# Turning B, K and V to token rows in one RWKV-7 / Conformer / MLP layer: the transposing mode of the tensor engine replaced by ordinary products with the identity

## The chip, the cores and the metric

One core of one Trainium2 chip runs the whole layer in one launch. The metric is the device time of an execution in microseconds; lower is better. The kernel before was timed three times.

## The reference, cut to what matters

640 tokens (512 latent, 128 context) of width 1024 pass through one layer:

```python
xn = _rmsnorm(x, norm1_g) * (1 + sc1) + sh1
proj = xn @ w_in                                    # r k v | conv inputs | gates
y_r = _rwkv_branch(...)                             # 8 heads of 64, two directions
y_c = _conv_branch(...)                             # GLU, depthwise conv of 31, LayerNorm, swish
x = x + g1 * ((sigmoid(gate_r) * y_r + sigmoid(gate_c) * y_c) @ w_o)
x = x + g2 * (square(relu(xn2 @ mlp_w1)) @ mlp_w2)

def step(S, inp):                                   # the scan inside the RWKV branch
    rt, wt, kt, vt, at, bt = inp
    sa = einsum('bhvk,bhk->bhv', S, at)
    S = S * wt[:, :, None, :] + sa[..., None] * bt[:, :, None, :] + vt[..., None] * kt[:, :, None, :]
    return S, einsum('bhvk,bhk->bhv', S, rt)
```

Everything is float32. Large products are done as three passes over operands split into two parts (`hi` and `lo`, type float32r); small ones are plain float32 products.

## The kernel before, in words

Channels lie on the 128 partitions, tokens along the free axis, in two halves of 320. The program has three stretches. First the statistics, the modulation and the low-rank projections. Then "phase 1": all projections of the modulated input (dense products, 128x128 weights times 128x320 inputs, tiles `ps_mm<-xh_t,wh_t` and the like), with the RWKV branch and the conv branch running between them. Last the output projection and the MLP, dense products alone.

The scan doesn't run token by token. For each pair of heads (four pairs, `p`) the tokens of each direction are cut into 20 chunks of 32. The jobs of a pair are:

- `operands` writes the decayed operands, B and K as tile `BK`, with channels on partitions.
- `gram` (L769) makes inner products of every chunk: for each chunk two products of 64x64, one per head, `ps_a<-ARGH_t,BK_w` or `ps_b<-ARGH_t,BK_w`. Head 0 lies on partitions 0 to 63 and writes partitions 64 to 127 of the PSUM bank; head 1 the other way.
- `inverse` solves a triangular system per chunk.
- `turn` (L892) makes copies of B and K with the tokens on the partitions (tile `BKt`): a product of each chunk's `BK` block as the weights with the identity as the moving operand, `ps_a<-cst_t,BK_w` or `ps_b<-cst_t,BK_w`. It has the same two heads on the same corners of the array as `gram`. Four chunks times two heads are issued together; ScalarE then copies the bank to `BKt`.
- `fold` (L924) multiplies with the inverse.
- `chain` (L1020) is the scan itself, 20 steps. At each step `values` (L990) turns the V of one chunk of each direction and head: four products with the identity, `ps_a<-cst_t,vS_w` and `ps_a<-cst_t,vr_w`.

Both kinds of product with the identity ask `turned_to` (L209) whether they may use the tensor engine's transposing mode. It answers yes where the output starts at partition 0: in `turn` that is head 1 of the pair, in `values` one of the four products (head 1, direction 1).

What sets the order: phase 1 is written out by a planner that runs when the program is built. Every job is a generator (a "lane") with an urgency; the loop at the end of phase 1 asks for the first lane that can go on, and puts dense products in wherever none can. It keeps its own clock of each engine (`now`, `free`). The method `mm` (L192) moves that clock for each product and counts columns for the array's clock; a product in the transposing mode counts as 2 cycles a column, any other float32 product as 4:

```python
cyc = math.prod(rhs.shape[1:]) * (1 if rhs.dtype == F32R else 2 if "is_transpose" in kw else 4)
```

The order that results is fixed for TensorE, VectorE and ScalarE; DMAs are queued on SyncE.

Of the kernel before, what the change touches and what calls it, by code (L numbers as in the profile page):

```python
# [17 lines left out]
P = 128  # L18
# [17 lines left out]
TTILES = (0, 128, 192)  # first of the 128 tokens of each tile of a half  # L36

# [20 lines left out]
NWR, NWH = 2, 3  # halves of weights on the way, and split ones  # L58
# model of the engines' times (us) that sets the order of issue in phase 1
YG, YT, YF = 4, 4, 4  # L60
LEAD, SEM, LOAD = 0.40, 0.2, 4.0
BURST, REFRESH = 0, 15.0  # products without others between, now and then (us), that bring it back to full rate
# urgency of the lanes (the lowest first)
URGENT = dict(scan=0, split=0.3, shift=1.45, post=1, side=0.9, solve=1, prep=1.5, lora=2, ada=4, out=4.5, branch=0.5, conv=1.6)
# least times (us) between products of a lane whose results leave by a DMA, or whose weights come by one
GAP_LORA, GAP_ADA = 1.5, 3.5
V_STEP = 20  # of the scan after which the projection of V that takes its place may be planned
GLU_AT = 12  # their place among the projections
TICK, ENTRY, QUOTA, CREDIT, DEBT = 3.413, 3060, 1.55, 200, 6000  # clock gate of the tensor engine: columns in a tick that keep it at full rate
CST_ID, CST_MASK, CST_SEL, CST_HSEL, CST_LATE = 0, 128, 256, 258, 260  # L70
NCST = 261
# blocks of K = 1024 weights, in the order of the packed array
# [4 lines left out]
def hybrid_step(ctx: ExitStack, tc: tile.TileContext, I, O):  # L77
# [8 lines left out]
    # Estimates of the engines' times, in us. Instructions of the tensor engine are issued at now[0].  # L86
# [3 lines left out]
    class Timed:  # L90
        """an engine that counts the time of its instructions"""
# [67 lines left out]
    late = cst[:, CST_LATE:CST_LATE + 1]  # 1 on the second half of each 32 partitions  # L159
# [9 lines left out]
    # products of nothing in particular bring the tensor engine's clock to its full rate  # L169
# [6 lines left out]
    hw0 = st([P, 16], "hw0")  # halves of decay_w0 and iclr_a0  # L176
    ka2 = st([P, 8], "ka2")   # k_a / 2 and 1 - k_a / 2
# [3 lines left out]
    def derive():  # L181
        """derived parameters"""
# [9 lines left out]
    def mm(out, lhsT, rhs, start=True, stop=True, **kw):  # L192
# [3 lines left out]
        overlap = 128 // m if m < 128 else 128 // rhs.shape[0]  # products in different rows or columns of the array  # L196
# [12 lines left out]
    def turned_to(q):  # L209
        """for a product with the identity: the transposing mode writes from partition 0 only"""  # L210
        return {} if q else dict(is_transpose=True)

    def split(hi, lo, src):
        """src = hi + lo, each with the mantissa of one float32r pass."""
        A.activation(hi, src, AF.Copy)
        V.tensor_tensor(out=lo, in0=src, in1=hi.bitcast(F32), op=ALU.subtract)

    # halves of weights: planned, on the way, split; tags of free places for raw and split ones, and of those in use
# [4 lines left out]
    def place(free_, b):  # L223
        """whether there is a free place for a half of block b; those of phase 1 are not for the blocks after it"""
        while free_ and free_[0] not in ("wr", "wh") and b >= B_WO:
            free_.popleft()
        return len(free_) > 0

    def prefetch():
        """load the next halves of weights"""  # L230
# [14 lines left out]
    def take():  # L245
        """split the next half of a weight"""
# [40 lines left out]
    def mm3(ps, w, xh, xl, n0, n1, ks, first=True, last_=True):  # L287
        """ps += W^T X over the k tiles ks of a half w of W (k0 ... of X): hi hi + hi lo + lo hi; yields after each k tile."""
# [21 lines left out]
    def dense(xh, xl, evac, k0=0, k1=KD, pre=None):  # L310
        """the next block of weights (k tiles k0 ... k1) times X; evac(h, a, b, psum) takes each token half.
        Yields whether the tensor engine has got something."""
# [26 lines left out]
    def root(r, ps, scale, op, c):  # L339
        """r = op(scale * ps, c) ** -0.5"""  # L340
        if op == "max":
            V.tensor_scalar(out=r, in0=ps, scalar1=c, scalar2=None, op0=ALU.max)
        else:
            V.tensor_scalar(out=r, in0=ps, scalar1=scale, scalar2=c, op0=ALU.mult, op1=ALU.add)
        G.tensor_tensor(out=r, in0=r, in1=mhalf[0:r.shape[0], 0:r.shape[1]], op=ALU.pow)

    def inv_rms(srcs, h, scale, c, tg, bc):
        """(scale * sum over channels of srcs + c) ** -0.5 for token half h, spread over the channels; bc(psum) takes it."""
# [13 lines left out]
    def inv_norm(src, scale, op, c, tg, bc):  # L362
        """op(scale * sum of src over the channels of each head, c) ** -0.5, spread over the head's channels;
        bc(a, b, psum) takes it."""
# [15 lines left out]
    csb = st([P, 2 * KD + 30], "csb")  # 32 columns from 2 k on: c and c_ctx first, the rest is not used  # L380
# [6 lines left out]
    def ada(cols, tag, raws):  # L387
        """columns of mod: silu(c) @ ada_w + ada_b, transposed; raws: (k0, k1, tile) of the weights"""
# [21 lines left out]
    amod = st([P, 16, 2], "amod")  # norm_g * (1 + scale)  # L410

    def modulate(xt, k, rs, norm, segs, xh, xl, r0=0):
        """tile k of segments of the modulated input, split; rs: from token r0 on"""
# [82 lines left out]
    halves.extend((B_RKV + 4, j) for j in range(2))  # of the first product of phase 1  # L496
# [11 lines left out]
    # low-rank inner activations  # L508
# [13 lines left out]
    def lora2(p):  # L522
        """outer products of the low-rank pairs: tanh halves of decay and rate, and the gate; to DRAM"""
        def product(which, a, b, outs):
            """rows, function and place of the result of each product"""
# [13 lines left out]
        for which in range(2):  # L539
            for a, b in HALVES:  # L540
                outs = []
                for d in range(2):
                    back = which == 0 and d == 1  # direction 1 of the decay runs backwards through the tokens
# [17 lines left out]
    def proj_shift(kind, p):  # L561
        """r, k or v of head pair p with the token shift."""
# [74 lines left out]
    def bsum(src, tags, out_f):  # L637
        """sums over the 64 channels of each head, spread over them."""
# [10 lines left out]
    def hold():  # L649
        """one lane at a time has the two banks"""  # L650
        while held[0]:
            yield 0.2
        held[0] = True
# [10 lines left out]
    def operands(p):  # L664
        """decayed, normalised operands of the chunks: A | R into ARGH, B and K into BK"""
# [19 lines left out]
        for d in range(2):  # L685
# [5 lines left out]
            # decay and in-context rate; direction 1 runs backwards through the tokens  # L691
# [51 lines left out]
    BKt = wt([P, 2, NY, 64], "BKt")  # B and K with the tokens on the partitions, over and under an identity  # L743
# [12 lines left out]
    # Units of a pair: head parity s and direction d. Channel rows of a unit: 64 s ... The other half holds  # L756
    # its U and V (B and K) rows, U in quadrant 2 (1 - s) + d and V in the other quadrant of that half.
# [11 lines left out]
    def gram(p):  # L769
        """masked inner products of every chunk into ARGH; raw ones of B and A into Gf; then the decay of a chunk onto BK"""  # L770
# [33 lines left out]
    def inverse(p):  # L804
        """N[t, chunk, s] = ((I - G)^-1)[t, s], by blocked forward substitution, one chunk per lane; to Gf
        (the lanes without a chunk keep a zero strict triangle)"""
# [7 lines left out]
        def mulred(jobs):  # L814
            """out[a, b] = sum_s g[a, b, s] n[a, b, s] of each job (out, g, n, dims)"""
# [23 lines left out]
        T21 = G2[:, 16:24, 0:16].rearrange("p s (i j) -> p i s j", i=2)  # (the part of G that is not used here)  # L839

        def merge(blocks, n, jb):
            """N21 = N22 G21 N11 for the blocks of size n at blocks"""
# [21 lines left out]
        # the blocks of 16 on the tensor engine: rows t of every unit in its quadrant  # L864
# [24 lines left out]
    # chunks of direction 0 and 1 from which groups of scan steps start, and their numbers of steps  # L889
    GROUPS = (((16, 0), 4), ((0, 4), 8), ((8, 12), 8))  # L890

    def turn(p):  # L892
        """B and K with the tokens on the partitions: rows of a head in the other half; and V backwards.
        A group of steps takes the place of the one of the last pair."""
        BK = grp[p]["BK"]
        for g, (c0, n) in enumerate(GROUPS):
# [4 lines left out]
            for i, ds in enumerate([(0, 1)] if n == 4 else [(0,), (1,)]):  # L901
                yield max(0.0, ends[-2] - now[0])
                ps = bank(BANKS[i]).rearrange("p (y c) -> p y c", c=64)
                for y in range(8):
                    at = 20 * ds[y // n] + c0[ds[y // n]] + y % n
                    for s in range(2):
                        lo, o = 64 * s, 64 - 64 * s
                        mm(ps[o:o + 64, y, :], BK[lo:lo + 64, at, :], ident[lo:lo + 64, lo:lo + 64], **turned_to(o))
# [15 lines left out]
    def fold(p):  # L924
        """N^T into the B rows of the state update and of the output"""
# [37 lines left out]
    def solve(p):  # L963
# [10 lines left out]
        if p == 3:  # the places of the inverse can have weights  # L974
# [3 lines left out]
    # rings of the scan: state, U and V rows  # L978
# [5 lines left out]
    def cidx(c, i):  # L984
        """chunk of each direction at step i of the latent ('l') or context ('c') scan"""
# [4 lines left out]
    def values(p, n):  # L990
        """the V rows of a step"""
        S, ps = SVU[p % 2][n % 2], grp[p]["ps"]
        for s, d in UNITS:
            lo, q, t = 64 * s, vq(s, d), 32 * cidx(*STEPS[n])[d]
            mm(ps[q:q + 32, d, :], (vr if d else rk[2, p])[lo:lo + 64, t:t + 32], ident[lo:lo + 64, lo:lo + 64],
               tile_position=(lo, q), **turned_to(q))
# [4 lines left out]
    def output(p, n):  # L1001
        """the outputs of a step"""
# [17 lines left out]
    def chain(p):  # L1020
# [14 lines left out]
        for n in range(20):  # L1035
# [14 lines left out]
            if n == 3:  # the latents start from the given states  # L1050
# [12 lines left out]
            end = S if n == 3 else Sn  # of the context: a result  # L1063
# [13 lines left out]
    def post(p):  # L1077
        """group norm of each head, bonus and gate; to DRAM"""
        y0, y = grp[p]["Y"], rk[2, p]  # V is not needed any more
# [572 lines left out]
```

## Time and profile before

| | |
|---|---|
| three timed runs | 1401.06, 1413.18, 1482.34 us |
| median | 1413.18 us |
| span of the profiled execution, first to last instruction | 1416.9 us |
| mean granted TensorE clock in it | 0.901 |
| TensorE products (PE), weight loads (PEld) | 1370.3 us (97%), 1165.0 us (82%) |
| VectorE (DVE), ScalarE (ACT), GpSimd (POOL) | 740.5 us (52%), 551.8 us (39%), 28.9 us (2%) |

The profile gives the span of its execution, not a time with what lies around it. Columns of a group's row: line, engine, operation, output and inputs, shapes, count of records, then busy us and mean ns of one, then the engine's idle time before them. In a timeline row the first number is the start in us from the span's start and the second the duration of the merged piece. In a row of stretches each engine has its busy us with the number of its records behind it, then come the granted clock (1.00 is full), the DMA share and GB/s. Line 193 is the matmul call in `mm` and line 106 the call through which VectorE, ScalarE and GpSimd instructions are recorded, so the tiles tell which instruction is meant.

### The profile page before, as it was taken

To read this page: it belongs to the slowest core of one execution; us is meant where nothing else is said; L and a number is where in the kernel's file an instruction comes from. 1 tells how busy PE (TensorE), PEld (TensorE's weight loads), DVE (VectorE), ACT (ScalarE), POOL (GpSimd) and SP (SyncE) were. 2 spreads that over 40 slices of the span, in tenths; PEclk is the share of its full clock that TensorE was granted. 3 is DMA by queue.
4 is the path that set the end of the run, shared out by engine and by line. 5 is a ranking of instruction groups with operands and counts; after the bars stand their busy time and mean duration, and the time that the engine had idled before them with its cause. 6 is when DMAs were issued, how large, how long until landed. Compare 5 with 4: busy or idle time off the path is not lost.

```text
span 1416.9 us, 31247 instructions
## 1 busy us (share of the span) xinstructions
PE 1370.3 (97%) x13122; PEld 1165.0 (82%) x13122; DVE 740.5 (52%) x1606; ACT 551.8 (39%) x1390; POOL 28.9 (2%) x21
## 2 busy tenths in 40 slices
PE   8999999999999999999999979999999999999997
PEld 5776677677777677776777879999999999999997
DVE  5445557663856557543574356565443343344344
ACT  4555336542644226422265522334442242242130
POOL 0100000000000000000000000000000000000000
PEclk9999869996988679655799999999999999999998
DMA  9455223120421134121322167321222222222222
GB/s 373 142 173 185 82 65 119 60 76 34 132 84 56 42 123 141 48 67 40 104 85 67 43 206 267 119 75 46 75 75 75 75 75 75 75 75 75 75 82 75
DMA packets 82572, 140.38 MB, mean 99 GB/s; under 512 B 17024, under 2 KB 31616, under 8 KB 82432
## 3 DMA queue, kind: packets, MB, share of 16 engines
q1 hardware_dynamic: 82432, 138.39, 29.4%
q8 instruction: 103, 1.69, 0.5%
q14 instruction: 37, 0.30, 0.1%
HBM read 113.52 MB, written 22.22 MB: 96 GB/s over the span
## 4 chain that ended last, share of the span: by engine, by line
PE 91%; DMA 4%; DVE 2%; issue 2%; ACT 1%; SPq 0%; POOL 0%; POOLq 0%; DVEq 0%; ACTq 0%
PE ps_mm L193 47%; PE ps_b L193 25%; PE ps_a L193 10%; PE ps_t L193 7%; PE ps_ad L193 3%; DMA adl_w<-in_adal 2%; DMA adar_s<-in_adaw 1%; DMA z<-tmp 1%; ACT tmp L106 0%; DVE kk_t L106 0%; DVE ARGH_t L106 0%; DVE vS_w L106 0%; DMA pg_t<-g 0%; DVE wl_t L106 0%; DVE rS_w L106 0%
## 5 line engine op out<-in xcount | busy, mean ns | idle before, releaser
L193 PE MATMUL ps_mm<-xh_t,wh_t 128*128 128x320 f32 x656 | 235.5, 359 | 2.0 <-ACT tmp L106 1.7
L193 PE MATMUL ps_mm<-xh_t,wl_t 128*128 128x320 f32 x656 | 232.2, 354 | 0.0
L193 PE MATMUL ps_mm<-xl_t,wh_t 128*128 128x320 f32 x656 | 230.9, 352 | 0.0
L106 ACT ACTIVATE svu_w<-ps_a 64x128 f32<-64x128 f32 x320 | 87.1, 272 | 171.5 <-PE ps_a L193 166.0
L193 PEld LDWEIGHTS ps_mm<-xh_t,wh_t 128*128 128x128 f32 x656 | 136.1, 208 | 21.1 <-issue 11.5
L193 PEld LDWEIGHTS ps_mm<-xl_t,wh_t 128*128 128x128 f32 x656 | 136.8, 209 | 15.2 <-issue 10.2
L193 PEld LDWEIGHTS ps_mm<-xh_t,wl_t 128*128 128x128 f32 x656 | 136.5, 208 | 13.6 <-issue 7.4
L106 ACT ACTIVATE wh_t<-wr_t 128x512 fp32r<-128x512 f32 x147 | 92.4, 629 | 138.7 <-PE ps_b L193 107.1
L106 DVE TENSOR_TENSOR wl_t<-wr_t,wh_t 128x512 fp32r<-128x512 f32 x147 | 100.9, 688 | 82.2 <-ACT wh_t L106 76.8
L106 DVE TENSOR_TENSOR svu_w<-ps_b,Dc_w 64x128 f32<-64x128 f32 x152 | 43.7, 288 | 80.8 <-PE ps_b L193 78.0
L106 DVE SCALAR_TENSOR_TENSOR cacc_w<-upad_w,par_t,cacc_w 128x640 f32<-128x640 f32 x90 | 79.2, 880 | 2.0 <-ACT cacc_w L106 0.2
L193 PE MATMUL ps_mm<-ARGH_t,wh_t 128*128 128x320 f32 x252 | 71.0, 321 | 2.7 <-ACT wh_t L106 1.7
L106 ACT ACTIVATE tmp<-ps_mm 128x320 f32<-128x320 f32 x80 | 34.8, 436 | 88.7 <-PE ps_mm L193 88.5
L193 PE MATMUL ps_mm<-ARGH_t,wl_t 128*128 128x320 f32 x196 | 63.1, 322 | 5.0 <-DVE wl_t L106 5.0
L106 ACT ACTIVATE BKt_w<-ps_a 32x512 f32<-32x512 f32 (+3 forms) x80 | 40.0, 503 | 55.8 <-PE ps_a L193 54.8
L106 ACT ACTIVATE mwh<-wr_t 128x512 fp32r<-128x512 f32 x49 | 30.9, 632 | 73.3 <-PE ps_b L193 69.9
L106 DVE TENSOR_TENSOR tmp<-tmp 128x320 f32<-128x320 f32 x64 | 31.2, 489 | 43.6 <-ACT tmp L106 43.5
L106 DVE TENSOR_TENSOR mwl<-wr_t,mwh 128x512 fp32r<-128x512 f32 x49 | 33.7, 690 | 37.9 <-ACT mwh L106 37.9
L106 DVE SCALAR_TENSOR_TENSOR ARGH_t<-ps_mm,mod_t,ARGH_t 128x320 f32<-128x320 f32 (+2 forms) x45 | 22.6, 511 | 57.9 <-PE ps_mm L193 57.9
L193 PE MATMUL ps_a<-cst_t,BK_w 64*64 64x64 f32 x288 | 52.2, 282 | 0.0
L193 PEld LDWEIGHTS ps_mm<-ARGH_t,wh_t 128*128 128x128 f32 x252 | 47.5, 199 | 3.8 <-ACT wh_t L106 1.9
L193 PEld LDWEIGHTS ps_a<-cst_t,BK_w 64*64 64x64 f32 x288 | 33.1, 146 | 20.5 <-issue 3.9
(374 smaller groups left out, 3156.7 us busy)
## 6 DMA issues: line engine op xcount, KB each, us to landing
wr_t<-in_w SPq DMA_DIRECT2D x222, 256.0 KB, 2.8
adl_w<-in_adal SPq DMA_DIRECT2D x64, 256.0 KB, 2.8
adar_s<-in_adaw SPq DMA_DIRECT2D x16, 512.0 KB, 8.4
ARGH_t<-in_x SPq DMA_DIRECT2D x8, 640.0 KB, 6.3
z<-tmp SPq DMA_DIRECT2D x32, 160.0 KB, 2.8
gate<-tmp SPq DMA_DIRECT2D x32, 160.0 KB, 2.1
tA_t<-z SPq DMA_DIRECT2D x8, 320.0 KB, 3.1
ath_t<-z SPq DMA_DIRECT2D x8, 320.0 KB, 4.8
```

Source lines behind the costliest of these rows:

```text
L106: return f(*args, **kw)
L193: PE.matmul(out=out, lhsT=lhsT, rhs=rhs, start=start, stop=stop, **kw)
```

## The change

`turned_to` is gone, and the two calls that used it pass nothing. All products with the identity in `turn` and `values` are ordinary float32 products, for both heads. Everything else in the diff is removed comments, which are left out here.

```diff
-    def turned_to(q):
-        """for a product with the identity: the transposing mode writes from partition 0 only"""
-        return {} if q else dict(is_transpose=True)
-
...
-                        mm(ps[o:o + 64, y, :], BK[lo:lo + 64, at, :], ident[lo:lo + 64, lo:lo + 64], **turned_to(o))
+                        mm(ps[o:o + 64, y, :], BK[lo:lo + 64, at, :], ident[lo:lo + 64, lo:lo + 64])
...
             mm(ps[q:q + 32, d, :], (vr if d else rk[2, p])[lo:lo + 64, t:t + 32], ident[lo:lo + 64, lo:lo + 64],
-               tile_position=(lo, q), **turned_to(q))
+               tile_position=(lo, q))
```

Because the planner counts the two modes differently, the written order changes too. TensorE in the first `turn` of the first pair (`BK_w` are B and K, `cst_t` the identity, `ps_a` the bank, `x8` four chunks of two heads), before:

```order
L193 MATMUL ps_mm<-xl_t,wh_t 128x320
L193 MATMUL ps_mm<-xh_t,wl_t 128x320
L193 MATMUL ps_a_1767<-cst_t,BK_w 64x64 x8
L193 MATMUL ps_mm<-xh_t,wh_t 128x320
L193 MATMUL ps_mm<-xl_t,wh_t 128x320
L193 MATMUL ps_a_1767<-cst_t,BK_w 64x64 x8
L193 MATMUL ps_mm<-xh_t,wl_t 128x320
```

These seven rows read the same in the changed program: here nothing moved, and a `turn` batch is eight products in both.

A little later on TensorE the orders part. Around a weight load for the modulation (`ps_ad<-adl_w,csb_t`, four products) stands, before:

```order
L193 MATMUL ps_mm<-xh_t,wh_t 128x320
L193 MATMUL ps_mm<-xl_t,wh_t 128x320
L193 MATMUL ps_mm<-xh_t,wl_t 128x320
L193 MATMUL ps_ad<-adl_w,csb_t 32x128 x4
L193 MATMUL ps_mm<-xh_t,wh_t 128x320
```

and in the changed program:

```order
L193 MATMUL ps_mm<-xh_t,wh_t 128x320
L193 MATMUL ps_mm<-xl_t,wh_t 128x320
L193 MATMUL ps_ad<-adl_w,csb_t 32x128 x4
L193 MATMUL ps_mm<-xh_t,wl_t 128x320
L193 MATMUL ps_mm<-xh_t,wh_t 128x320
```

The small products moved ahead of one dense product.

On ScalarE, where the first pair's scan begins (`ARGH_t` and `BKt_w` are written by `fold`, `svu_w` by the scan, `wh_t` is a split weight, `u_t` and `rS_w` are the evacuated projection of r), before:

```order
L106 ACTIVATE BKt_w<-ps_a_2366 32x512
L106 ACTIVATE mod_t<-ps_ad,par_t 128x2
L106 ACTIVATE BKt_w<-ps_a_2366 32x512
L106 ACTIVATE svu_w<-ps_a_2390 64x2x64 x2
L106 ACTIVATE BKt_w<-ps_a_2366 32x512 x2
L106 ACTIVATE svu_w<-ps_a_2390 64x2x64 x4
L106 ACTIVATE tmp<-ps_mm 128x320
```

and in the changed program:

```order
L106 ACTIVATE BKt_w<-ps_a_2363 32x512
L106 ACTIVATE ade_t<-ps_ad 128x128
L106 ACTIVATE wh_t<-wr_t 128x512
L106 ACTIVATE BKt_w<-ps_a_2363 32x512 x3
L106 ACTIVATE svu_w<-ps_a_2358 64x2x64 x8
L106 ACTIVATE Y_w<-ps_t 128x32 x2
```

The scan's first copies (`svu_w`) moved behind the last of `fold`'s copies of that group, and one more split of a weight stands ahead of them. From there on, pieces of a few instructions differ all through phase 1; the counts of batches (40 of eight in `turn`, 80 of four in `values`) don't.

## The prediction

> **What bounds the kernel now.** I read the page's busy table first, then its slices, then its chain.
>
> ```profile
> span 1416.9 us, 31247 instructions
> PE 1370.3 (97%) x13122; PEld 1165.0 (82%) x13122; DVE 740.5 (52%) x1606; ACT 551.8 (39%) x1390; POOL 28.9 (2%) x21
> ...
> PEclk9999869996988679655799999999999999999998
> ...
> PE 91%; DMA 4%; DVE 2%; issue 2%; ACT 1%; SPq 0%; POOL 0%; POOLq 0%; DVEq 0%; ACTq 0%
> ```
>
> TensorE (PE) is busy for 97% of the span and holds 91% of the chain that ended last: it stands idle for only 46.6 us, so a microsecond taken out of its queue is nearly a microsecond of the kernel. The clock row is the second thing to see: between a tenth and a half of the span it falls to 5 and 6 again and again. PE is then just as "busy", but slower. Next, the PE groups of the products with the identity:
>
> ```profile
> L193 PE MATMUL ps_a<-cst_t,BK_w 64*64 64x64 f32 x288 | 52.2, 282 | 0.0
> L193 PE MATMUL ps_b<-cst_t,BK_w 64*64 64x64 f32 x192 | 40.0, 314 | 0.0
> L193 PE MATMUL ps_a<-cst_t,vr_w 64*32 64x64 f32 x240 | 39.2, 243 | 0.0
> L193 PE MATMUL ps_a<-cst_t,vS_w 64*32 64x64 f32 x320 | 26.2, 245 | 0.0
> ```
>
> The program has 320 products in `turn` and 320 in `values`; the trace has 480 and 560 records. So an ordinary float32 product leaves two records and a transposing one leaves one: half of `turn` (160) and a quarter of `values` (80) are transposing. A batch in `turn` is four chunks times two heads: 12 records, 40 batches in all.
>
> The mean of a record hides the price, because records overlap. The timeline shows it: from a batch's start to the start of what follows. Three extracts: `turn` at full clock and at half clock; `gram`, which is eight ordinary products of the same 64x64 shape on the same two corners of the array, at both clocks; and one run of dense products at each.
>
> ```profile
> 158.65 1.78 PE L193 MATMUL ps_a<-cst_t,BK_w 64*64 64x64 f32 x12
> 160.36 0.41 PE L193 MATMUL ps_mm<-xh_t,wl_t 128*128 128x320 f32 x1
> ...
> 167.30 2.63 PE L193 MATMUL ps_a<-cst_t,BK_w 64*64 64x64 f32 x12
> 169.86 0.63 PE L193 MATMUL ps_mm<-xh_t,wl_t 128*128 128x320 f32 x1
> ...
> 133.21 0.68 PE L193 MATMUL ps_b<-ARGH_t,BK_w 64*64 64x64 f32 x16
> 133.82 0.41 PE L193 MATMUL ps_mm<-xl_t,wh_t 128*128 128x320 f32 x1
> ...
> 427.17 1.12 PE L193 MATMUL ps_a<-ARGH_t,BK_w 64*64 64x64 f32 x16
> 428.21 0.63 PE L193 MATMUL ps_mm<-xh_t,wl_t 128*128 128x320 f32 x1
> ...
> 157.09 0.31 PE L193 MATMUL ps_mm<-xl_t,wh_t 128*128 128x320 f32 x1
> 157.24 0.31 PE L193 MATMUL ps_mm<-xh_t,wl_t 128*128 128x320 f32 x1
> ...
> 170.82 0.47 PE L193 MATMUL ps_mm<-xh_t,wl_t 128*128 128x320 f32 x1
> 171.09 0.47 PE L193 MATMUL ps_mm<-xh_t,wh_t 128*128 128x320 f32 x1
> ```
>
> `turn`: 1.71 us at full clock, 2.56 at half. `gram`, with four records more: 0.61 and 1.04. A dense product every 0.15 and 0.27. Fewer records take 2.8 times as long: what costs is the alternation of the two modes, in which nothing overlaps.
>
> Then the clock by stage, with cuts laid where it changes, and the first and last `turn` records in each stretch:
>
> ```profile
> core 0: us, PE busy (x) PEld busy (x) DVE busy (x) ACT busy (x) POOL busy (x), PEclk, DMA share, GB/s
> 61.00:164.10 103.10, 94.98 (x785) 72.00 (x783) 53.86 (x120) 52.17 (x122) 3.91 (x2) 1.00 0.55 173
> 164.10:198.50 34.40, 34.40 (x147) 23.57 (x146) 9.70 (x34) 7.11 (x15) 0.00 (x0) 0.50 0.06 21
> 259.90:352.10 92.20, 91.27 (x913) 64.46 (x913) 49.25 (x125) 35.98 (x114) 2.28 (x1) 0.80 0.18 59
> 413.50:437.40 23.90, 22.63 (x206) 16.72 (x207) 9.82 (x26) 10.32 (x36) 0.00 (x0) 0.50 0.16 54
> 471.50:512.50 41.00, 41.00 (x175) 28.59 (x175) 15.48 (x51) 8.92 (x19) 2.36 (x1) 0.50 0.10 34
> 512.50:580.80 68.30, 64.88 (x1232) 49.70 (x1228) 48.83 (x90) 37.20 (x111) 0.00 (x0) 1.00 0.43 133
> 580.80:649.00 68.20, 68.20 (x602) 48.52 (x603) 28.93 (x65) 21.72 (x75) 0.00 (x0) 0.50 0.16 49
> 655.90:690.00 34.10, 33.17 (x149) 23.77 (x149) 11.39 (x46) 7.76 (x15) 1.96 (x1) 0.50 0.11 36
> ...
> L193 PE MATMUL ps_a<-cst_t,BK_w x24: 218/242/267, 408.7 to 413.3; 64*64 64x64 f32 x24
> L193 PE MATMUL ps_a<-cst_t,BK_w x48: 218/309/366, 467.9 to 493.1; 64*64 64x64 f32 x48
> L193 PE MATMUL ps_a<-cst_t,BK_w x24: 218/242/267, 576.3 to 580.6; 64*64 64x64 f32 x24
> ```
>
> A slow stretch begins within 6 us of the first batch of a `turn`: 158.65 and 164.1, 408.7 and 413.5, 467.9 and 471.5, 576.3 and 580.8. I take the same for the two others (from 259.9 and 655.9). The `gram` batch at 133.21 stands in a stage at full clock (61.0 to 164.1, 1.00).
>
> **The change, part by part.** Nothing is added but 240 records (160 + 80); PE's instructions keep their number, and the copies out of PSUM keep theirs. The reordering that comes with it (below) leaves 40 batches of eight in `turn` and 80 of four in `values`.
>
> First, `turn`. After the change a batch is `gram`'s pattern with the identity as moving operand, so I price it at 0.61: 40 x (1.71 - 0.61) = **44 us** at full clock. Bounds: no gain (1.71), or half of `gram`'s (0.31), which would give 56. I take `gram`, the same shape to the last number.
>
> Second, `values`. Now and the nearest group of four ordinary products, at full clock:
>
> ```profile
> 438.31 0.25 PE L193 MATMUL ps_a<-cst_t,vS_w 64*32 64x64 f32 x2
> ...
> 438.41 0.38 PE L193 MATMUL ps_a<-cst_t,vr_w 64*32 64x64 f32 x2
> 438.71 0.41 PE L193 MATMUL ps_mm<-xh_t,wl_t 128*128 128x320 f32 x1
> ...
> 578.50 0.32 PE L193 MATMUL ps_a<-svu_w,ARGH_t 128*32 128x64 f32 x8
> 578.75 0.42 PE L193 MATMUL ps_t<-ARGH_t,svu_w 128*64 128x32 f32 x8
> ```
>
> 0.40 us now (only the last of the four transposes), 0.25 for the four products of the scan's first step: 80 x 0.15 = **12 us**. Bounds: nothing, or all but one pitch of a dense product, 80 x 0.25 = 20.
>
> Third, the clock, the largest term. The slow stretches tied to a `turn` hold 34.4 + 36.9 (92.2 at 0.80) + 23.9 + 41.0 + 68.2 + 34.1 = 238.5 us at half clock. The `turn` products alone (busy us, records, clock) in the three stretches that hold no `gram`:
>
> ```profile
> 164.10:198.50 34.40, 20.87 (x96) 0.50 0.06 21
> 471.50:512.50 41.00, 16.81 (x78) 0.50 0.10 34
> 655.90:690.00 34.10, 15.88 (x73) 0.50 0.11 36
> ```
>
> That is 53.6 us of `turn`, which at full clock would be 1.71/2.56 of it: 17.8 saved (the further saving down to 0.61 is in the first term). The other 184.9 us are dense products (0.15/0.27 = 0.55) and small ones (0.61/1.04 = 0.58); at 0.57 they save 79.5. Together **97 us**. Bounds: nothing (the clock falls as before) and 109, with the four slow stretches of 7 us elsewhere gone as well (27.3 x 0.43 = 12). I take 97, because the fall follows the first batches of a `turn` wherever I looked, and `gram`, interleaved with dense products in the same way, doesn't cause it.
>
> Here two places of the Trainium skill's page "TensorE: Matmul & The Clock Gate" pull apart. Its section "Why this matters for your kernels" lets the clock fall after an idle gap of some 3 us; the rows disagree, since PE is busy for 34.40 of 34.40 us at clock 0.50, and by that rule there is no gap to close, the third term is zero and rival (a) below holds. Its part 4, "PE-mode transpose", says that the transposing mode doesn't count as PE activity in the same way; by that the third term is real. The trace sides with the second.
>
> What is late next: with PE faster, DVE and ACT have less cover. At 0.57 of its time, and `turn` at 0.61 a batch, the stretch from 471.5 (6.5 batches, 16.8 us of it) shrinks to 4.0 + 13.8 = 17.8 us for 15.5 us of DVE work, 87%; that from 164.1 to 12.6 us for 9.7, 77%; that from 580.8 to 38.9 for 28.9, 74%. At full clock today, from 512.5, DVE is at 71% and PE idles 3.4 of 68.3 us, 5%. I charge **10 us** of new waits: 5% of the 100 us that these stretches keep, doubled for the dense one.
>
> The order: the planner counts a transposing product as half an ordinary one, so its clock now runs on a little more in each batch and later choices differ by one dense product here and there, ACT's copies between the first scan steps with them, and SP's loads. In the first `turn` nothing moves. I cost the reordering at nothing; it can go either way by some 10 us, since PE's waits of all kinds sum to 46.6.
>
> Sum against the profiled span: 1416.9 - 44 - 12 - 97 + 10 = 1273.9. Its own time outside the span isn't given; the median of the three runs, 1413.2, lies 3.7 below the span, and I forecast **1270 us**.
>
> **The rivals.** (a) The clock falls as before, because the stage is thin in dense products and not because of the mode. Then `turn` saves 1.1 us in some 20 batches and 2.56 - 1.04 = 1.52 in the other 20, `values` 12 to 16: 52 + 14 = 66, and the time is 1347. For it: the stretch from 580.8 holds no `turn` after its start and stays slow for 68 us, so a thin mix alone can keep the clock down. Against: `gram`'s stage.
>
> (b) The clock recovers in part, or DVE binds: one stretch like that from 580.8 in a new place costs 68.2 x 0.43 = 29 us, so one gives about 1300 and two 1330.
>
> (c) Slower: it is the ordinary product with the identity that is dear, at its place in `turn`, and the transposing one is nearly free. Then eight cost 8 x 1.71/4 = 3.42 a batch: 40 x 1.71 = 68 more, `values` a third of 0.40 more in 80 steps, 11; 1413 + 79 = 1492. It decides from 0.21 us for an ordinary product (1.71 / 8). Against: `gram`'s eight take 0.61, 0.08 each. The Trainium skill stands on this side: "Perfetto Trace Analysis", section "Transposes", asks for the transposing mode in place of a standard matmul, because it skips the arithmetic. No row here shows a transposing product alone; the 1.71 against 0.61 speaks against the rule for alternating modes.
>
> (d) That nothing comes of it, the gain in PE being lost to new waits of the scan: 1413.
>
> **How the numbers follow.** Forecast, 1235 to 1295 around 1270: 0.70. (b) 0.14, (a) 0.08, (d) 0.05, (c) 0.03. The range from 1235 (all upper bounds of the gains short of the full extra clock, 1413 - 56 - 20 - 97 = 1240, with some luck in the order) to 1330 holds the forecast and most of (b), some 8 in 10. About 2% (1385) is what a measurement here can tell. Below it lie the forecast, (a) and (b): faster 0.92; (d): same 0.05; (c): slower 0.03.
>
> **What would show it.** `turn` batches of 16 records, 0.6 us from start to start; `values` of 8 records, about 0.25; a clock row without the 5 and 6 of the fifth to the twentieth slice; the records of these products up by 240. Wrong if a `turn` batch takes over 1 us at full clock, if the clock still falls within 6 us of a `turn`, or if PE's idle time grows by more than 30 us.

## The result, and the profile after

The changed kernel takes 1285.74 us (median of four runs, 1274.04 to 1294.05) against 1425.96 for the kernel before (four runs): a ratio of 0.911, 95% interval 0.894 to 0.928. In a second comparison it was 1289.86 against 1435.94, 0.908 (0.900 to 0.917). The kernel before scatters from 1401 to 1482 us in all comparisons of this text, the slower the lower its granted clock (0.914 in a run of 1405 us, 0.865 in one of 1467), so the ratios and intervals are taken from the faster runs of each kernel, the medians from all. The profiled execution took 1274.04 us with a span of 1272.3, 144.6 us less than the span before.

From the page of the changed kernel, the busy row, the clock row and the chain that ended last:

```profile
PE 1219.7 (96%) x13362; PEld 1069.1 (84%) x13362; DVE 739.8 (58%) x1606; ACT 549.7 (43%) x1390; POOL 28.2 (2%) x21
...
PEclk9999998979999999999999999999999999999998
...
PE 86%; DMA 5%; DVE 4%; issue 2%; ACT 2%; SPq 1%; POOL 0%; POOLq 0%; DVEq 0%; ACTq 0%
```

PE has 240 records more and 151 us less of busy time; the 5s and 6s of its clock are gone (the lowest digit is a 7). DVE's and ACT's work is the same to some two microseconds, only their shares rose. The groups of the products with the identity:

```profile
L193 PE MATMUL ps_a<-cst_t,BK_w 64*64 64x64 f32 x384 | 16.4, 224 | 0.0
L193 PE MATMUL ps_b<-cst_t,BK_w 64*64 64x64 f32 x256 | 10.9, 224 | 0.0
L193 PE MATMUL ps_a<-cst_t,vr_w 64*32 64x64 f32 x320 | 24.7, 232 | 0.0
L193 PE MATMUL ps_a<-cst_t,vS_w 64*32 64x64 f32 x320 | 24.7, 232 | 0.0
```

640 and 640 records in place of 480 and 560. A `turn` batch, a step's `values` and the product behind each, in the timeline:

```profile
158.10 0.68 PE L193 MATMUL ps_a<-cst_t,BK_w 64*64 64x64 f32 x16
158.71 0.41 PE L193 MATMUL ps_mm<-xh_t,wl_t 128*128 128x320 f32 x1
...
228.03 0.25 PE L193 MATMUL ps_a<-cst_t,vS_w 64*32 64x64 f32 x2
...
228.12 0.22 PE L193 MATMUL ps_a<-cst_t,vr_w 64*32 64x64 f32 x2
228.27 0.42 PE L193 MATMUL ps_mm<-xl_t,wh_t 128*128 128x320 f32 x1
```

0.61 us in place of 1.71, and 0.24 in place of 0.40. One row of phase 1 for each kernel, before and after (us of the stretch; then busy us of PE, PEld, DVE, ACT, POOL with the count of records; the granted clock; DMA share and GB/s):

```profile
61.00:834.00 773.00, 746.06 (x8910) 560.80 (x8909) 426.62 (x962) 339.58 (x965) 19.52 (x10) 0.83 0.29 91
...
61.00:834.00 773.00, 735.06 (x10058) 601.99 (x10051) 517.29 (x1162) 387.17 (x1067) 20.53 (x12) 0.98 0.38 118
```

At 0.83 such a stretch holds 2 x 0.17 x 773 = 263 us at half clock, at 0.98 it holds 31. In the same 773 us the changed kernel gets through 1148 more PE records; up to 240 of them are only the second records of the products that no longer transpose.

### The profile page after: what moved, and what is told of

It is laid out like the page before. It is cut to its first block, busy times and chain, and to the rows that moved or that the text cites. A ratio compares the mean times of both kernels' runs of the same rounds, so it can differ in the third digit from the quotient of the medians.

```text
span 1272.3 us, 31723 instructions
## 1 busy us (share of the span) xinstructions
PE 1219.7 (96%) x13362; PEld 1069.1 (84%) x13362; DVE 739.8 (58%) x1606; ACT 549.7 (43%) x1390; POOL 28.2 (2%) x21
## 4 chain that ended last, share of the span: by engine, by line
PE 86%; DMA 5%; DVE 4%; issue 2%; ACT 2%; SPq 1%; POOL 0%; POOLq 0%; DVEq 0%; ACTq 0%
PE ps_mm L193 46%; PE ps_b L193 24%; PE ps_a L193 7%; PE ps_t L193 7%; PE ps_ad L193 2%; DMA adl_w<-in_adal 2%; DMA adar_s<-in_adaw 1%; DMA z<-tmp 1%; ACT tmp L106 1%; DVE Gt_w L106 0%; DMA prod_w<-in_w 0%; DVE ARGH_t L106 0%; DVE kk_t L106 0%; DVE wl_t L106 0%; DVE vS_w L106 0%
## 5 line engine op out<-in xcount | busy, mean ns | idle before, releaser
L193 PE MATMUL ps_mm<-xh_t,wh_t 128*128 128x320 f32 x648 | 217.5, 336 | 1.8 <-ACT tmp L106 1.8
L193 PE MATMUL ps_mm<-xh_t,wl_t 128*128 128x320 f32 x648 | 213.9, 330 | 0.0
L193 PE MATMUL ps_mm<-xl_t,wh_t 128*128 128x320 f32 x648 | 213.2, 329 | 0.0
L193 PEld LDWEIGHTS ps_mm<-xh_t,wh_t 128*128 128x128 f32 x648 | 123.6, 191 | 21.2 <-issue 11.7
L193 PEld LDWEIGHTS ps_mm<-xl_t,wh_t 128*128 128x128 f32 x648 | 123.4, 190 | 13.7 <-issue 9.0
L193 PEld LDWEIGHTS ps_mm<-xh_t,wl_t 128*128 128x128 f32 x648 | 123.5, 191 | 9.9 <-issue 4.4
L193 PE MATMUL ps_mm<-xl,wh_t 128*128 128x320 f32 x140 | 43.9, 314 | 0.0
L193 PE MATMUL ps_b<-ARGH_t,wl_t 128*128 128x320 f32 x140 | 43.6, 312 | 0.0
```

Source lines behind the costliest of these rows:

```text
L193: PE.matmul(out=out, lhsT=lhsT, rhs=rhs, start=start, stop=stop, **kw)
```

## The experiments

**Order against modes.** The planner counts a transposing product as half an ordinary one, so the change also moved instructions. Two runs take the two apart. The order of the changed kernel with the old modes, made by counting 4 cycles a column always:

```diff
-        cyc = ... (1 if rhs.dtype == F32R else 2 if "is_transpose" in kw else 4)
+        cyc = ... (1 if rhs.dtype == F32R else 4)
```

> The written order of the changed kernel, with the two modes of the kernel before (head 1 of turn and one of four products of values transposing). Theory M (the modes cost the time, by 1.71 us batches of turn and the clock that falls behind them): as slow as before, ratio 0.98 to 1.02, turn batches of 12 records and 1.71 us at full clock, half-clock stretches of over 200 us in sum. Rival O (the reordering brought the gain): ratio near 0.91, few half-clock stretches although turn stays at 1.71 us.

And the order of the kernel before with the new modes:

```diff
-        PE.matmul(out=out, lhsT=lhsT, rhs=rhs, start=start, stop=stop, **kw)
+        PE.matmul(out=out, lhsT=lhsT, rhs=rhs, start=start, stop=stop, **{k: v for k, v in kw.items() if k != "is_transpose"})
```

> The written order of the kernel before, with ordinary products for both heads. Theory M: ratio 0.89 to 0.93, turn batches of 16 records and 0.61 us, half-clock stretches under 60 us in sum. Rival O: ratio 0.97 to 1.0; turn at 0.61 us brings its 44 us at most and the clock still falls behind each turn.

Order alone: 1405.3 us, ratio 0.988 (0.981 to 0.996). Modes alone: 1278.3 us, 0.899 (0.893 to 0.904). The stretch from 150 to 700 us, which holds all `turn` batches, for the kernel before, order alone and modes alone:

```profile
150.00:700.00 550.00, 539.26 (x6647) 397.15 (x6646) 313.22 (x719) 226.29 (x664) 11.77 (x5) 0.78 0.25 79
150.00:700.00 550.00, 537.70 (x6881) 397.27 (x6879) 320.80 (x735) 228.43 (x671) 10.91 (x5) 0.80 0.26 80
150.00:700.00 550.00, 528.90 (x8597) 415.86 (x8593) 388.82 (x887) 295.54 (x870) 15.60 (x8) 0.98 0.33 101
```

The clock follows the modes (0.80 and 0.98), not the order. The new order is some 20 us better with the old modes. With the new modes it isn't better than the old order: medians of 1286 and 1290 against 1278, in different comparisons, and the intervals of the ratios overlap (0.911 and 0.908 against 0.899). Theory M holds, O falls.

**Which of the two places.** Both with the planner's counts of the changed kernel; `turned_to` is kept in `values` alone, then in `turn` alone.

```diff
# turn_only
-  mm(ps[o:o + 64, y, :], BK[lo:lo + 64, at, :], ident[lo:lo + 64, lo:lo + 64], **turned_to(o))
+  mm(ps[o:o + 64, y, :], BK[lo:lo + 64, at, :], ident[lo:lo + 64, lo:lo + 64])
# values_only
-  tile_position=(lo, q), **turned_to(q))
+  tile_position=(lo, q))
```

> The order of the changed kernel; turn is ordinary for both heads, one of the four products of values still transposes. Theory M: the 12 us of values are missing and nearly nothing else, ratio 0.91 to 0.93 (about 1298 us), values at 0.40 us. Rival V (the single transposing product in each of 80 scan steps is what pulls the clock down): half-clock stretches stay over 150 us and the ratio is 0.95 or more.

> The order of the changed kernel; values is ordinary, head 1 of turn still transposes. Theory M: 12 us less than before, ratio 0.98 to 1.0, values at 0.25 us, half-clock stretches still over 200 us and beginning within 6 us of a turn. Rival V: half-clock stretches mostly gone, ratio 0.95 or less.

`turn` alone: 1299.7 us, 0.912 (0.905 to 0.918). `values` alone: 1401.5 us, 0.985 (0.976 to 0.994). The same stretch, in that order:

```profile
150.00:700.00 550.00, 528.55 (x8398) 411.89 (x8398) 378.31 (x869) 287.13 (x855) 14.92 (x8) 0.96 0.30 94
150.00:700.00 550.00, 534.46 (x7137) 396.86 (x7133) 327.36 (x741) 233.69 (x684) 10.91 (x5) 0.80 0.26 82
```

`turn` holds the clock and most of the gain: 106 us against order alone. What `values` is worth is not shown by the times: the medians differ by 4 us at the old clock (1401.5 against 1405.3) and by 10 to 14 where the clock stands (1299.7 against 1289.9 and 1285.7), but the intervals of the ratios overlap (0.985 against 0.988; 0.912 against 0.911 and 0.908). Rival V falls: 80 single transposing products in the scan leave the clock at 0.96.

**The alternation against the mode.** In each batch head 0's four products first, then head 1's four; modes as before.

```diff
-  for y in range(8):
-      for s in range(2):
...
+  for y0 in range(0, 8, YT):
+      for s in range(2):
+          for y in range(y0, y0 + YT):
```

> The order of the changed kernel and the modes of the kernel before, but in each turn batch the four products of head 0 (ordinary) come first and then the four of head 1 (transposing): one change of mode in a batch in place of eight. Theory M1 (the alternation is dear, not the mode): a batch near 1.0 us at full clock (four ordinary ones one behind the other 0.43, one change of 0.15, four transposing ones some 0.3, the way out 0.15), half-clock stretches shorter, ratio 0.92 to 0.95. Rival M2 (each transposing product is dear by itself): 1.4 us or more a batch, ratio 0.97 or more. The rule that the transposing mode is the cheaper one: the four transposing ones take less than the four ordinary ones, which the records show.

1303.9 us, 0.919 (0.907 to 0.932), although as many products transpose as before. A batch, then its eight ordinary and its four transposing records in narrow cuts of the timeline:

```profile
160.39 1.02 PE L193 MATMUL ps_a<-cst_t,BK_w 64*64 64x64 f32 x12
161.33 0.41 PE L193 MATMUL ps_mm<-xh_t,wl_t 128*128 128x320 f32 x1
...
160.39 0.67 PE L193 MATMUL ps_a<-cst_t,BK_w 64*64 64x64 f32 x8
...
160.99 0.41 PE L193 MATMUL ps_a<-cst_t,BK_w 64*64 64x64 f32 x4
...
150.00:700.00 550.00, 534.52 (x8182) 414.63 (x8177) 375.58 (x864) 285.94 (x851) 14.91 (x8) 0.97 0.30 93
```

0.94 us in place of 1.71. The four ordinary products take 0.60 from their start to that of the first transposing one; the four transposing ones take 0.34 to the next dense product's start. So the mode is not dear by itself. M1 holds, M2 falls: what cost 1.71 us was to change mode eight times. The clock stands at 0.97 although 160 products of `turn` still transpose. The Trainium skill's rule ("Perfetto Trace Analysis", section "Transposes": use the transposing mode rather than a standard matmul) holds here for products in a row of their kind, 0.34 against 0.60 us for four, each with about 0.15 of way out. Interleaved with ordinary products they turned it round, and for the whole kernel no run shows the grouped transposing mode to be better than ordinary products (1303.9 us against 1285.7 and 1289.9 of the changed kernel, whose `values` are ordinary too).

The same grouping with ordinary products throughout:

> The changed kernel with the four products of head 0 ahead of the four of head 1 in each turn batch, all ordinary: as the run with grouped heads, but without the transposing mode. If what the changed kernel gains inside a batch is that the two heads overlap in two corners of the array, the overlap is gone here: 16 records one behind the other, 0.058 us each as head 0's eight stand in the run with grouped heads, 0.93 us and the way in and out, 1.0 to 1.1 us a batch against 0.95 there; 40 x 0.45 us more than the changed kernel, ratio 0.91 to 0.93. If the overlap is of no matter, a batch stays near 0.61.

```profile
163.49 0.96 PE L193 MATMUL ps_a<-cst_t,BK_w 64*64 64x64 f32 x16
164.38 0.41 PE L193 MATMUL ps_mm<-xh_t,wl_t 128*128 128x320 f32 x1
...
150.00:700.00 550.00, 533.53 (x8425) 418.91 (x8425) 375.29 (x863) 286.77 (x854) 14.92 (x8) 0.93 0.30 93
```

0.89 us a batch, less than the 1.0 to 1.1 expected, but 0.28 more than with the heads interleaved: the changed kernel's 0.61 needs the two heads side by side in two corners of the array. 1308.4 us (1288.0 to 1311.8) against a median of 1441.7 for the kernel before; this run has no ratio with an interval. The longer batches account for 40 x 0.28 = 11 us of the 19 to 23 above the changed kernel; in the profiled run the clock is lower too, 0.93.

**The clock: the mode or the thin stretch.** Two runs from both sides. First the kernel before, unchanged but for eight useless dense products ahead of each batch of `turn`, into the place that the batch overwrites; and the same in the changed kernel, for the price of those products.

```diff
+NDUM = 8
...
+  if y % YT == 0:
+      for _ in range(NDUM):
+          PE.matmul(out=ps[:, y:y + YT, :], lhsT=xh_(0)[:, 0:128], rhs=xh_(0)[:, 0:256], start=True, stop=True)
```

> The kernel before, in its own order, with eight useless dense products (128x128 weights, 256 columns) ahead of each turn batch, into the place in PSUM that the batch then overwrites: 40 x some 1.0 us of additional work. Theory C (the clock falls because too few columns pass through the array in a stretch of 3 to 4 us): the clock stays up, 97 us less for 40 us more, ratio 0.95 to 0.98, turn still 1.71 us. Rival T (the transposing mode itself pulls the clock down, however dense the rest is): the clock falls as before, ratio 1.02 to 1.05.

> The changed kernel with the same eight useless dense products ahead of each turn batch: what they cost where the clock stands at full. All theories: 40 x some 1.0 us, about 1325 us, ratio to before 0.92 to 0.95. If they cost far less (under 15 us), the stretch of turn isn't bound by the tensor engine.

```profile
160.97 1.11 PE L909 MATMUL ps_a<-xh_t 128*128 128x256 f32 x8
162.01 1.78 PE L194 MATMUL ps_a<-cst_t,BK_w 64*64 64x64 f32 x12
163.72 0.41 PE L194 MATMUL ps_mm<-xh_t,wl_t 128*128 128x320 f32 x1
...
150.00:700.00 550.00, 534.26 (x7493) 412.85 (x7493) 332.83 (x752) 236.10 (x696) 11.77 (x5) 0.94 0.28 85
```

The kernel before, with 40 x 1.04 = 42 us of useless work, is faster than without: 1386.4 us, 0.975 (0.962 to 0.988). Its batches still alternate and still take 1.71 us, and the clock stands at 0.94 in place of 0.78. It isn't cured altogether: three slow stretches, 51 us in sum, still begin within 2 us of a `turn` batch (at 265.2, 429.0 and 507.5 us). In the changed kernel the same work costs 32 to 36 us (1321.5 us, 0.932, 0.922 to 0.943). Theory C holds, T falls. The clock that came back was therefore worth some 67 to 81 us: 35 (a ratio of 0.975) to 45 (the medians 1431.4 and 1386.4), and the price of the useless work on top. The clock rows give the same: 0.16 x 2 x 550 x 0.43 = 76.

Then the other side: no transposing product anywhere, but one tiny product of the whole array between the chunks.

```diff
   at = 20 * ds[y // n] + c0[ds[y // n]] + y % n
+  PE.matmul(out=ps[:, y, 0:2], lhsT=ident, rhs=ident[:, 0:2], start=True, stop=True)
```

> The changed kernel (no transposing product anywhere) with one tiny ordinary product of the whole array (128x128 weights, 2 columns) ahead of each chunk's two products in turn, into a place that they then overwrite: 160 products that pass almost no columns, but break the row of equal tiles as the alternation of modes did. Theory C (the clock follows the columns that pass, whatever the mode): a turn batch takes 1.5 to 2.0 us with no more columns than at 0.61, half-clock stretches begin behind turn again, over 150 us in sum, ratio 0.97 to 1.01. Rival T (only the transposing mode pulls the clock down): a batch takes as long, the clock stays up, 40 x 1.0 to 1.4 us more than the changed kernel, ratio 0.92 to 0.95.

```profile
157.90 0.28 PE L902 MATMUL ps_a<-cst_t 128*128 128x2 f32 x2
158.10 0.33 PE L193 MATMUL ps_a<-cst_t,BK_w 64*64 64x64 f32 x4
...
159.83 0.33 PE L193 MATMUL ps_a<-cst_t,BK_w 64*64 64x64 f32 x4
160.09 0.41 PE L193 MATMUL ps_mm<-xh_t,wl_t 128*128 128x320 f32 x1
...
150.00:700.00 550.00, 536.01 (x7044) 427.48 (x7041) 308.48 (x714) 223.05 (x658) 10.92 (x5) 0.80 0.25 76
```

A batch takes 2.19 us, more than the 1.5 to 2.0 expected, the clock falls to 0.80 and the time is 1428.6 us, ratio 1.010 (1.000 to 1.020), at the upper end of what theory C allowed: the whole gain is lost, though PE transposes nothing. 40 x 1.58 = 63 us of batches and 0.18 x 2 x 550 x 0.43 = 85 us of clock on top of 1286 give 1434.

**Fewer changes between dense and small products.** `YG, YT, YF = 8, 8, 8` in the changed kernel; then that with the planner's old counts, beside the changed kernel itself on the same chip.

> The changed kernel with gram, turn and fold issued eight chunks at a time in place of four: some 60 groups of small products between dense ones become some 30. Theory W (a change between dense and small products costs about 0.2 us at full clock, as the first dense pitch of 0.25 in place of 0.15 behind a group and 0.24 ahead of one show): 5 to 12 us less than the changed kernel. Rival: the longer groups hold up dense products or thin out the columns and the clock falls more often: the same or up to 20 us more.

> The changed kernel once more, as the measure for the run beside it on the same chip: ratio 0.90 to 0.92 to the kernel before.

> Ordinary products for both heads, the planner's counts of the kernel before, and groups of eight chunks in gram, turn and fold. If the few us that each of the two showed alone against the changed kernel (1278 and 1282 against 1286) are real and add up: 6 to 12 us less than the changed kernel beside it. If they were noise: within 5 us of it.

Eight chunks at a time: 1281.9 us, 0.902 (0.892 to 0.913), not told apart from the changed kernel. Theory W's 5 to 12 us are neither shown nor ruled out. Both together: 1278.6 us (six runs, 1273.8 to 1280.2), 0.901 (0.896 to 0.907), against 1289.9 (1274.3 to 1292.7) beside it: 11 us less in the medians, with ranges that overlap. The old order with the new modes had 1278.3 without the larger groups, so a gain by the larger groups isn't shown.

## Why the prediction was right, and where its reason was not

- **`turn`, 44 us.** 0.61 us was taken from `gram` and 0.61 measured, in all 40 batches. Right.
- **`values`, 12 us.** 0.24 against 0.25 forecast, in place of 0.40: right by the timeline, 80 x 0.16 = 13 us. The times of whole runs don't resolve it.
- **The clock, 97 us.** The size was right: 263 - 31 = 232 us of half clock went, at 0.43 a term of 100. The filled kernels put what they brought back at 67 to 81, with some slow stretches left in them. The reason given was wrong. "The fall follows the first batches of a `turn`" was true, but I set the mode against the thin stretch in rival (a) and took the side of the mode. The runs show the thin stretch: the clock stands with the transposing products in place once dense ones fill in (0.94), or once they are grouped (0.97), and falls with none (0.80). The alternation only made the batch long. So the Trainium skill's statement weighed there ("TensorE: Matmul & The Clock Gate", part 4, "PE-mode transpose": the transposing mode doesn't count as PE activity in the same way) isn't what decided here. Rival (a) had the cause right and its result wrong, since it took the stretch to stay as thin as before. By an estimate from the rows, the 16 records of a batch are worth 16 x 64 / 2 = 512 columns of the whole array in 0.61 us, the 12 of before 384 in 1.71. Whether it is the few columns or the time in which the array stands empty between changes, these runs don't separate. An idle gap isn't what began the slow stretches of the kernel before. PE was busy throughout ahead of each of the six that the prediction lists, as in these two:

```profile
408.00:413.50 5.50, 5.50 (x47) 3.80 (x47) 2.88 (x6) 0.98 (x6) 1.79 (x1) 1.00 0.09 33
576.00:580.80 4.80, 4.80 (x44) 3.22 (x43) 1.90 (x3) 1.17 (x6) 0.00 (x0) 1.00 0.19 72
```

- **New waits, 10 us.** PE's idle time grew from 46.6 to 52.6 us (1272.3 - 1219.7). Right in kind: the largest waits are for DMA and DVE. Two of them stand at the start of the two longest slow stretches that are left in phase 1 of the profiled execution, both over 28 us behind the last `turn` batch:

```profile
200.81 1.34 PE L193 MATMUL ps_t<-kk_t,cst_t 128*64 128x320 f32 x4 [3.12 <-DVE kk_t L106]
...
269.70 0.30 PE L193 MATMUL ps_mm<-xh_t,wh_t 128*128 128x320 f32 x1
272.20 0.66 PE L193 MATMUL ps_ad<-adl_w,csb_t 128*32 128x128 f32 x8 [2.20 <-DMA adl_w<-in_adal]
...
255.00:269.70 14.70, 14.49 (x227) 10.84 (x227) 11.21 (x27) 8.94 (x32) 0.00 (x0) 1.00 0.31 83
270.00:291.00 21.00, 18.80 (x206) 14.00 (x209) 8.85 (x24) 7.29 (x24) 0.00 (x0) 0.59 0.15 47
```

  PE waits 2.20 us for a load of modulation weights and comes back at half clock, where it stays for 17 us over scan steps, `gram` and dense products, a mix that had run at 1.00 just before. Behind the wait of 3.12 us it stays at half for some 7. So the clock came back lower from both waits, and the shorter one cost more than itself: 17 us at half clock are 17 x 0.43 = 7 us.
- **The reordering, nothing.** Some 20 us better with the old modes, twice the 10 allowed; in the medians 8 to 12 worse with the new, which isn't clear of noise.
- **The sum.** 143 us forecast against the profiled span, 144.6 measured. To agree that closely was luck: the measured parts, 44 + 13 + 100 - 6 = 151, are good to some 6 us, and the runs of the changed kernel spread over 20. The forecast of 1270 lies 16 us under the median. 13 of them come from the base, since the median before rose from 1413 to 1426 with the fourth run, and 3 from the gain, 140 in the medians. The ratio forecast, 1270 / 1413 = 0.899, lies in the interval.

Rival (c), that ordinary products are the dear ones, fell with 0.61 a batch, (d) with the result. Of (b) something is left: the runs of the changed kernel spread over 20 us, the slower with the lower clock (1274 us at 0.985, 1294 at 0.967).

## What to carry to other kernels

A mean duration says nothing of what pipelined products cost: read from the start of a group to the start of what follows, and compare it with a group of the same shape elsewhere in the kernel. Don't alternate modes or tile shapes product by product; group them, or give up the mode, even if it is the shorter one in a row of its kind. Where the clock row drops, estimate what passes through the array rather than how busy it is: here a batch that was long and thin slowed all its neighbours, and even useless dense work paid for itself.

## What the runs showed of the hardware

- An ordinary float32 product leaves two records, a transposing one leaves one: 640 records for the 320 products of `turn` when all are ordinary, 480 when half of them transpose.
- Changing between transposing and ordinary products of the same tile is about as dear as changing the tile shape: eight products take 1.71 us with a change at each and 0.94 us with one, and four pairs take 2.19 us with a tiny product of another shape ahead of each. From record to record, a change of either kind takes 0.15 to 0.18 us in these traces (158.90 to 159.08 in the kernel before, 158.50 to 158.68 with the tiny products), where records of one kind in one corner follow each 0.06.
- In the kernel before, the granted clock fell in stretches where PE was busy without a gap. Estimates from the rows, records x 64 columns x half of the rows: 225 columns a us in a `turn` batch of 1.71 us and 234 in one of 2.19, in kernels where the clock fell (0.78 and 0.80); 839 in one of 0.61, where no fall followed a batch in the profiled execution; and (8 x 256 + 384) / 2.75 = 884 with the useless products, where three falls were left (0.94). No run here shows where between 234 and 839 the limit lies.
- Once down, the clock can stay there: a mix of scan steps, `gram` and dense products ran at 1.00 from 255.0 to 269.7 us in the changed kernel and at half clock for 17 us behind a wait of 2.20; a mix of the same kinds kept it at half for 68 us in the kernel before (from 580.8).
